# Opening of a transformer trunk: adaLN map loaded by column quarters, context projected as quarters land, token squares summed by TensorE

## Chip, cores and metric

One core of a Trainium2 chip (trn2) runs the whole program. The metric is the device time of one execution in microseconds; of several runs the median is taken. Engines: PE is TensorE (PEld its weight loads), DVE is VectorE, ACT is ScalarE, POOL is GpSimd, SP is SyncE, which issues the DMAs here.

## The reference, cut to what matters

Two layers over 1024 latent tokens and 256 context tokens of 1024 channels, in fp32. Each layer is an attention and a gated convolutional FFN, each behind an RMS norm that is modulated by a vector (adaLN): one map `w_mod[i]` of 1024 x 6144 gives six vectors of 1024 channels for the latents (from `c`) and six for the context (from `c_ctx`). The change touches the start of layer 0:

```
mod = silu_c @ w_mod[i] + b_mod[i]
mod_c = silu_cc @ w_mod[i] + b_mod[i]
sh1, sc1, gt1, sh2, sc2, gt2 = jnp.split(mod[:, None, :], 6, axis=-1)
...
h = modulate(rmsnorm(x, g_attn[i]), sh1, sc1)        # h * (1 + scale) + shift
hc = modulate(rmsnorm(ctx, g_attn[i]), sh1c, sc1c)
q, k, v = attn_inputs(h, w_in, gq, gk, n_kv)          # h @ w_qkv, 1024 x 3072
q_c, k_c, v_c = attn_inputs(hc, w_in, gq, gk, n_kv, with_q=not last)
```

Before the first projection of layer 0 can start, the shift and scale vectors (the first 2048 of the 6144 columns of `w_mod[0]`, 8 MiB) must be there, and the tokens must be normalised and modulated.

## The kernel before, in words

Tokens lie transposed: 128 channels on the partitions, 8 channel tiles (k), and three chunks of tokens in the free dimension: chunk 0 and chunk 1 of 512 latents, chunk 2 of 256 context tokens. Every fp32 factor of a large matmul is split into a high part (fp32r) and a low part, and a product is three matmuls: hi x hi, lo x hi, hi x lo. For weights this gives `whi` (ACT) and `wlo` (DVE or POOL), for tokens `h0hi`, `h0lo`, and `h0chi`, `h0clo` for the context.

The order of the work is planned by `Sched` (line 61), a list scheduler that runs when the program is built. Each operation has an engine, an assumed duration, the tokens it reads and writes, a key (smaller goes first) and the buffers it takes and gives back. The planner plays the operations through and then emits them; `InOrder` (line 39) binds each engine to that order. So the order on an engine is fixed; at run time an instruction only waits for its own inputs, and all that stand behind it on its engine wait with it.

The opening is the planner `sa` (lines 787 to 932):

- DMA order: context tokens (two halves of 0.5 MiB), `cpad` (the two silu vectors), `bmod`, `gn`, latent chunk 0 (four quarters of 0.5 MiB), the map in eight tiles `wm` of 128 rows x 2048 columns (1 MiB each), three weight slabs of the first head pair (0.375 MiB), latent chunk 1 (four of 0.5 MiB), the fourth slab.
- `mod_mm` (297): for each row tile of the map and each of the two vectors, 4 matmuls of 256 columns into 32 partitions each; all eight row tiles are summed in PSUM, so no column of the result is complete before the last row tile. Then `cp` copies the two sums (`modsb`), PE transposes them (`modt`), and `mod_finish` (280) adds the bias and multiplies with the norm's gain into `modc`.
- `stats(c)` (842): ACT squares each of the 8 channel tiles of a chunk; DVE adds the eight squares into `nsum`; PE multiplies `nsum` with a column of 1/1024 (`invd`), one matmul of one column per 128 tokens (`nps`), 2 for the context and 4 for chunk 0. From that DVE and POOL make 1/sqrt (`nv`, `ny`, `nt`), DVE puts it on diagonals (`dg`), PE spreads it over the partitions (`nps<-dg,ones`), and DVE multiplies the tokens with it (`x<-x,nps`).
- `apply(c)` (899): per channel tile `x` is modulated (ACT or DVE), copied to the high part and subtracted for the low part. All wait for the whole `modc`.
- The four slabs are split into `whi` and `wlo`. Two tiles of the `wlo` ring hold the context tokens until then, so slabs 2 and 3 wait for the context's `h0clo`.

Then the planner `sc` plans layer 0's attention, from the time `T0` (1163) on: eight head pairs, each with q, k, v projections (`plan_na_qkv`, 973) of ten token tiles of 128 in the order context (8, 9), chunk 0 (0 to 3), chunk 1 (4 to 7), each 24 matmuls of 384 columns (`mm`), beside the attention of the pair. The context's projection thus begins after the opening. `plan_norm` (632) normalises chunk 1 meanwhile (`sums`, `n1v`, `n1y`, `t`, `n1lo`).

Of the kernel before, what the change touches and what calls it, by code (L numbers as in the profile page):

```python
# [11 lines left out]
F32 = mybir.dt.float32  # L12
# [5 lines left out]
P = 128  # L18
D = 1024
KT = 8  # L20
# [205 lines left out]
@with_exitstack  # L226
def trunk_kernel(ctx, tc, xperm, xseq, cc, wmod, bmod, gnorm, na_wqkv, na_gq, na_gk, na_bias, na_wo,
                 sw_wqkv, sw_gq, sw_gk, sw_sink, sw_wo, rope_c, rope_s, band, w_up, conv, w_down, out):
# [109 lines left out]
    def t_act(n):  # L338
        return 0.094 + n / 1200.0
# [448 lines left out]
    slabs = Slabs(na_wqkv, WL0)  # L788

    with tc.tile_pool(name="x0", bufs=1, reuse_waits="tile") as xp, \  # L790
            tc.tile_pool(name="lw0", bufs=2, reuse_waits="tile") as lw, \
            tc.tile_pool(name="ps0", bufs=1, space=PS, reuse_waits="tile") as ps:
        xs = [hpool.tile([P, KT, 512], F32, tag="hhi", name="x0", bufs=2),
              Parts([lo_part("x1", F32) for _ in range(4)], 2),
              Parts([wring.tile([P, 1024], F32, tag="wlo", name="x2").rearrange("p (k t) -> p k t", k=4) for _ in range(2)], 4)]
        h = [hi_lo("h0", 0), None, hi_lo("h0", 2)]


        sa = Sched(dict(raw=3, w=WBUFS, sq=2, nsum=1, n=2))
# [11 lines left out]
        accs, raws = [None] * 2, [None] * KT  # L811
        for kt in range(KT):
            def load(e, kt=kt):
                raws[kt] = xp.tile([P, 2, 1024], F32, tag="wm", name=f"wm{kt}", bufs=KT)
                dma.dma_start(raws[kt].rearrange("p v c -> p (v c)"), wmod[0, kt * P:(kt + 1) * P, 0:2 * D])

            def mm(e, kt=kt):
                for v in range(2):
                    if kt == 0:
                        accs[v] = ps.tile([P, 512], F32, tag="mod", name=f"mod{v}", bufs=2)  # L820
                    mod_mm(accs[v], kt, raws[kt][:, v, :], kt == 0, kt == KT - 1)
            sa.op("dma", t_mb, load, writes=[("wm", kt)], key=4 + kt)
            sa.op("pe", 0.86, mm, reads=[("wm", kt)], writes=[("acc", v) for v in range(2)], key=0)
        for v in range(2):
            J = {}

            def cp(e, v=v, J=J):
                J["sb"] = xp.tile([P, 256], F32, tag="modsb", name="modsb0", bufs=2)
                act.activation(J["sb"], accs[v][:, :256], AF.Copy)

            def tr(e, v=v, J=J):
                J["gen"] = mod_finish(0, v, J["sb"], lambda: ps.tile([P, 512], F32, tag="modt", name="modt", bufs=2))
                next(J["gen"])

            def fin_(e, J=J):
                for _ in J["gen"]:
                    pass
            sa.op("act", 0.28, cp, reads=[("acc", v)], writes=[("sb", v)], key=-1)
            sa.op("pe", 0.43, tr, reads=[("sb", v)], writes=[("modt", v)], key=-1)
            sa.op("dve", 0.2 + 0.2 * v, fin_, reads=[("modt", v), ("bmod",), ("gn",)], writes=[("modc", v)], key=-1)  # L840

        def stats(c, key):
# [5 lines left out]
            for k in range(KT):  # L848
                def sq(e, k=k):
                    J["s", k] = lw.tile([P, 512], F32, tag="sq" if k else "nsum", name="sq" if k else "nsum", bufs=2 if k else 1)  # L850
# [4 lines left out]
                sa.op("act", t_act(n), sq, reads=[("x", c, k)], writes=[("sq", c, k)] if k else [("sums", c)], key=key + k,  # L855
                      acq=[("sq", ("sq", c, k), 1)] if k else [("nsum", ("nsum", c), 1)])
                if k:
                    sa.op("dve", t_dve(n), add, reads=[("sq", c, k), ("sums", c)], writes=[("sums", c)], key=key + k,
                          rel=[("sq", c, k)])

            def mp(e):
                J["mp"] = ps.tile([P, 512], F32, tag="n", name="nps", bufs=2)
                for i in range(nt):
                    pe.matmul(J["mp"][:, i:i + 1], J["s", 0][:, i * P:(i + 1) * P], invd, start=True, stop=True)
            sa.op("pe", 0.22 * nt, mp, reads=[("sums", c)], writes=[("mp", c)], key=key, acq=[("n", ("mp", c), 1)],
                  rel=[("nsum", c)])

# [14 lines left out]
            def dg(e):  # L882
                J["dg"] = lw.tile([P, 512], F32, tag="sq", name="dg", bufs=2)
# [35 lines left out]
        stats(0, 30)  # L919
        apply(2, 50)  # L920
        apply(0, 60)
        slabs.n_ahead = 4
        for j in range(4):

            free = [("h", 2, k) for k in range(4 * (j - 2), 4 * (j - 1))] if j > 1 else []
            sa.op("dma", 0.94, lambda e, j=j: slabs.load(j), writes=[("raw", j)], key=20 + j if j < 3 else 40,
                  acq=[("raw", ("raw", j), 2)])
            sa.op("act", t_act(768), lambda e, j=j: slabs.hi(j), reads=[("raw", j)] + free, writes=[("wh", j)],
                  key=50 + 2 * j, acq=[("w", ("w", j), 1)], rel=[("raw", j)])
            sa.op("dve", 0.87, lambda e, j=j: slabs.lo(j, e), reads=[("raw", j), ("wh", j)] + [("modc", 1)] * (j > 0),  # L930
                  writes=[("wl", j)], key=50 + 2 * j, rel=[("raw", j)])
        sa.run()
# [5 lines left out]

    def ps_alloc(pool_):

        return lambda tag, dt: pool_.tile([P, 512], dt, tag=tag, name=tag, bufs=PSB[tag])

    psa = ps_alloc(ps)
    SBUFS, PTB = 5, 2
# [28 lines left out]
    def plan_na_qkv(n):  # L973
# [188 lines left out]

    T0 = max(sa.at(("h", 2, 0)), sa.at(("wl", 0)))
    for tok, was in ([(("h0", c, k), ("h", c, k)) for c in (2, 0) for k in range(KT)] + [(("x1", k), ("x", 1, k)) for k in range(KT)]
                     + [(("wl", j), ("wl", j)) for j in range(4)]):
# [5 lines left out]
    for hp in range(HP):  # L1171
        for j in range(4):
            if 4 * hp + j >= slabs.n_ahead:
                slabs.plan(sc, 4 * hp + j, NT * hp + QKEY, NT)
            else:
                sc.hold("w", ("w", j), NT)
        for k in range(NT):
# [49 lines left out]
    plan_oproj0()  # L1227
    sc.run({e: max(0.0, sa.free.get(e, 0.0) - T0) for e in ("act", "dve", "pool")})
    ph.close()
# [878 lines left out]
    ps = ph.enter_context(tc.tile_pool(name="psa1", bufs=1, space=PS, reuse_waits="tile"))  # L2108
    psa = ps_alloc(ps)
    
    kkl1 = fin.tile([P, T], F32R, name="kkl1")
# [286 lines left out]
def layout(i):  # L2398
# [7 lines left out]
    a["cc"] = np.stack([cols(i["c"][0]), cols(i["c_ctx"])], axis=-1)  # L2406
    a["wmod"] = i["w_mod"]
    a["bmod"] = i["b_mod"].reshape(2, 6, 8, P).transpose(3, 0, 1, 2)
    a["gnorm"] = np.stack([i["g_attn"], i["g_ffn"]], 1).reshape(2, 2, 8, P).transpose(3, 0, 1, 2)
# [14 lines left out]
    for g in range(NKV):  # L2424
# [16 lines left out]

_INS = ["xperm", "xseq", "cc", "wmod", "bmod", "gnorm", "na_wqkv", "na_gq", "na_gk", "na_bias", "na_wo",
        "sw_wqkv", "sw_gq", "sw_gk", "sw_sink", "sw_wo", "rope_c", "rope_s", "band", "w_up", "conv", "w_down"]
# [22 lines left out]
```

## Time and profile before

| what | value |
|---|---|
| median of 3 runs | 2849.25 us (2848.09 to 2849.77) |
| the profiled execution | 2851.74 us |
| its span on the core | 2850.0 us |
| mean granted clock of TensorE | 0.989 |
| busy PE, DVE, ACT, POOL | 2784.4, 2324.1, 1713.2, 400.1 us |

The page of the profile gives sums over the span; a row of the view by stretches gives the busy time of each engine, the granted clock and the DMA share between two times; a row of the timeline gives start, duration, engine, line, operation, output<-input, partitions x columns and the count of merged instructions, and in brackets the idle time before it and what ended that. Nearly all operations bear line 51, the line of the helper that records them; so they are told apart by the names of their tiles.

### The profile page before, as it was taken

Reading aid. Unit: us, or ns where it says so; the run is one execution under the profiler, and the core shown is the slowest. Engines: PE = TensorE matmul, PEld = TensorE weight load, DVE = VectorE, ACT = ScalarE, POOL = GpSimd, SP = SyncE. Lnnn points to the kernel's source line nnn. Section 1 sums busy time; section 2 is a strip of 40 time slices with the busy share of each in tenths; the row PEclk is TensorE's granted clock in tenths of the full one; section 3 lists DMA queues with packets and bytes.
Section 4 is the critical chain, followed back from the end, with each engine's and each line's share of the span. In section 5 each row is a group of like instructions: output and inputs, shape, how many; then the busy total and the mean of one; then the engine's idle time right before and its main releaser. Section 6 shows DMA issues by size and latency. Waiting matters only on the chain.

```text
span 2850.0 us, 46124 instructions
## 1 busy us (share of the span) xinstructions
PE 2784.4 (98%) x16344; PEld 2455.3 (86%) x16344; DVE 2324.1 (82%) x5243; ACT 1713.2 (60%) x3382; POOL 400.1 (14%) x675
## 2 busy tenths in 40 slices
PE   6999999999999999999999999999999999999999
PEld 5999999998789987777788888999987788888887
DVE  7888888888688687877797787999987988888757
ACT  5877777778456554444454457888873554455443
POOL 1222212223000000000010006455520000000000
PEclk9999999999999999999999999999999999999999
DMA  6222222314745544444375551010234323324745
GB/s 247 65 95 80 83 67 75 96 60 125 250 142 192 183 162 140 154 142 160 135 258 194 181 169 29 13 34 16 73 128 138 116 105 111 111 93 149 253 148 182
DMA packets 140953, 367.20 MB, mean 129 GB/s; under 512 B 21425, under 2 KB 34225, under 8 KB 139313
## 3 DMA queue, kind: packets, MB, share of 16 engines
q1 hardware_dynamic: 140720, 364.25, 38.1%
q8 instruction: 129, 2.11, 0.3%
q14 instruction: 104, 0.84, 0.1%
HBM read 297.21 MB, written 66.98 MB: 128 GB/s over the span
## 4 chain that ended last, share of the span: by engine, by line
PE 69%; DVE 4%; ACT 2%; issue 1%; DMA 1%; DVEq 0%; ACTq 0%; SPq 0%
PE ua L51 17%; PE dn L51 15%; PE uc L51 13%; PE mm L51 6%; PE oacc L51 4%; PE ud L51 4%; PE pt L51 3%; PE pv L51 2%; PE dnc L51 2%; PE s L51 2%; DVE S L51 1%; PE mod L51 1%; ACT S L51 1%; DVE ptlo L51 1%; DVE x L51 0%
## 5 line engine op out<-in xcount | busy, mean ns | idle before, releaser
L51 ACT ACTIVATE whi<-wraw 128x512 fp32r<-128x512 f32 (+1 forms) x264 | 212.6, 806 | 203.6 <-PE uc L51 62.7
L51 DVE TENSOR_TENSOR wlo<-wraw,whi 128x512 fp32r<-128x512 f32 (+1 forms) x264 | 239.2, 907 | 45.3 <-ACT whi L51 44.8
L51 DVE TENSOR_TENSOR ptlo<-pt,pthi 128x512 fp32r<-128x512 f32 (+2 forms) x384 | 223.2, 595 | 48.6 <-ACT pthi L51 45.0
L51 PE MATMUL dn<-ghi,wlo 128*128 128x512 f32 x616 | 242.4, 394 | 0.0
L51 PE MATMUL dn<-ghi,whi 128*128 128x512 f32 x616 | 242.4, 394 | 0.0
L51 PE MATMUL dn<-glo,whi 128*128 128x512 f32 x616 | 242.3, 393 | 0.0
L51 ACT ACTIVATE pthi<-pt 128x512 fp32r<-128x512 f32 (+2 forms) x384 | 195.1, 524 | 71.1 <-PE pt L51 61.1
L51 ACT ACTIVATE S<-S,m 128x640 f32<-128x640 f32 (+3 forms) x288 | 220.8, 768 | 22.7 <-DVE m L51 19.6
L51 DVE SCALAR_TENSOR_TENSOR u<-c,cv,u 128x1023 f32<-128x1023 f32 x176 | 223.2, 1279 | 6.8 <-ACT u L51 5.8
L51 ACT ACTIVATE whi<-s 128x1024 fp32r<-128x1024 f32 (+1 forms) x120 | 113.3, 945 | 191.4 <-PE uc L51 137.4
L51 ACT ACTIVATE ghi<-graw 128x512 fp32r<-128x512 f32 x154 | 96.4, 631 | 190.2 <-PE dn L51 108.4
L51 PE MATMUL pt<-idr,S 128*128 128x128 f32 x1280 | 199.2, 278 | 6.8 <-DVE sm L51 2.6
L51 PE MATMUL mm<-whi,h0hi 128*128 128x384 f32 x512 | 181.1, 354 | 0.4 <-ACT qraw L51 0.4
L51 DVE TENSOR_TENSOR glo<-graw,ghi 128x512 fp32r<-128x512 f32 x154 | 105.4, 688 | 83.8 <-ACT ghi L51 76.4
L51 PE MATMUL mm<-wlo,h0hi 128*128 128x384 f32 x512 | 172.3, 337 | 0.0
L51 PEld LDWEIGHTS pt<-idr,S 128*128 128x128 f32 x1280 | 153.5, 143 | 17.4 <-DVE ptlo L51 3.9
L51 DVE TENSOR_TENSOR wlo<-s,whi 128x1024 fp32r<-128x1024 f32 (+1 forms) x120 | 129.6, 1080 | 40.6 <-ACT whi L51 40.5
L51 POOL TENSOR_TENSOR qy<-qv,mhalf 128x4 f32<-128x4 f32 (+2 forms) x120 | 126.2, 1052 | 227.0 <-DVE qv L51 197.0
L51 PE MATMUL pv<-ptlo,v 128*128 128x256 f32 (+1 forms) x688 | 153.9, 297 | 1.2 <-DVE ptlo L51 1.2
L51 PE MATMUL pv<-pthi,v 128*128 128x256 f32 (+1 forms) x688 | 147.7, 287 | 4.1 <-DVE osb L51 3.0
L51 PE MATMUL ua<-t12hi,whi 128*128 128x512 f32 x352 | 138.7, 394 | 5.5 <-ACT t12hi L51 3.9
L51 POOL TENSOR_TENSOR n1y<-n1v,mhalf 128x4 f32<-128x4 f32 (+1 forms) x9 | 9.2, 1025 | 953.3 <-DVE n1v L51 950.7
(315 smaller groups left out, 8906.4 us busy)
## 6 DMA issues: line engine op xcount, KB each, us to landing
wraw<-in_w_up_dram SPq DMA_DIRECT2D x132, 512.0 KB, 3.4
wm<-in_wmod_dram SPq DMA_DIRECT2D x80, 512.0 KB, 4.0
wraw<-in_w_down_dram SPq DMA_DIRECT2D x44, 512.0 KB, 3.5
graw<-g_dram SPq DMA_DIRECT2D x44, 512.0 KB, 4.4
wraw<-in_w_down_dram SPq DMA_DIRECT2D x88, 256.0 KB, 3.0
graw<-g_dram SPq DMA_DIRECT2D x66, 256.0 KB, 2.8
slab<-in_na_wqkv_dram SPq DMA_DIRECT2D x32, 384.0 KB, 3.7
woraw<-in_na_wo_dram SPq DMA_DIRECT2D x24, 512.0 KB, 4.4
```

What stands on the lines that cost most here:

```text
L51: r = f(*a, **k)
```

## The change

The first 2048 columns of layer 0's map are laid out anew on the host (`wmod0`) as four quarters: quarter q holds, for all 1024 rows, columns 256q to 256q+255 of both shift and scale. A quarter (2 MiB) is loaded in two halves of 4 row tiles, 8 KB a partition as before. When a quarter is in, its two channel tiles (2q and 2q+1) of shift and scale are complete: 16 matmuls per quarter (even and odd row tiles in different partition groups, added later by DVE), a copy, two transposes, five DVE operations. `apply` for channel tile k waits for quarter k // 2 alone. The DMA order is context, slab 0, quarter 0, chunk 0, slab 1, quarter 1, slab 2, quarter 2, slab 3, quarter 3, chunk 1.

The context tiles 8 and 9 of head pair 0 are projected within the opening: for each slab j (channel tiles 2j, 2j+1) 12 matmuls as soon as slab j and the modulated channel tiles are there, into two PSUM banks (`psq`) that the attention goes on with; `plan_na_qkv` leaves them out. Chunk 0 follows as before.

The squares are not added by DVE: PE multiplies each square tile with `invd` and sums over the 8 channel tiles in PSUM; 4 square buffers instead of 2 and a sum. The context tokens get tiles of their own, outside the `wlo` ring. In the order that results on PE, 16 one-column matmuls of the context stand first, then 8 of quarter 0, the context's broadcast, 8 of quarter 0, 4 one-column matmuls of chunk 0, the transposes of quarter 0, 24 one-column matmuls of chunk 0, 8 of quarter 1, the last 4 one-column matmuls, then projections of the context in four parts among the rest of the quarters.

```diff
+        SQB = 4
+        sa = Sched(dict(raw=3, w=WBUFS, sq=SQB, n=2, mod=2, modt=2))
-        for c, parts, key in ((2, 2, 0), (0, 4, 2), (1, 4, 30)):
+        for c, parts, key in ((2, 2, 0), (0, 4, 6), (1, 4, 30)):
...
+        def plan_quarter(q):
+            J = {}
+            for hf in range(2):
+                def load(e, hf=hf):
+                    if hf == 0:
+                        J["raw"] = xp.tile([P, KT, 2, 256], F32, tag="wm", name=f"wm{q}", bufs=4)
+                    dma.dma_start(J["raw"][:, 4 * hf:4 * hf + 4].rearrange("p k v c -> p (k v c)"),
+                                  wmod0[q, :, 2048 * hf:2048 * hf + 2048])
+                sa.op("dma", t_mb, load, writes=[("wm", q, hf)], key=4 + 4 * q + 0.5 * hf)
+                def mm(e, hf=hf):
...
+                    for kt in range(4 * hf, 4 * hf + 4):
+                        for v in range(2):
+                            g = 2 * v + kt % 2
+                            pe.matmul(J["acc"][32 * g:32 * g + 32, :256], cpad[:, kt, :], J["raw"][:, kt, v, :],
+                                      start=kt < 2, stop=kt > 5, skip_group_check=True)
...
-                def add(e, k=k):
-                    dve.tensor_tensor(out=J["s", 0][:, :n], in0=J["s", 0][:, :n], in1=J["s", k][:, :n], op=ALU.add)
+                def mp(e, k=k):
...
+                    for i in range(nt):
+                        pe.matmul(J["mp"][:, i:i + 1], J["s", k][:, i * P:(i + 1) * P], invd, start=(k == 0 and i == 0),
+                                  stop=(k == KT - 1), skip_group_check=True)
+                sa.op("act", t_act(n), sq, reads=[("x", c, k)], writes=[("sq", c, k)], key=key + k, acq=[("sq", ("sq", c, k), 1)])
+                sa.op("pe", 0.22 * nt, mp, reads=[("sq", c, k)], writes=[("mp", c)], key=key + k,
+                      acq=[("n", ("mp", c), 1)] if k == 0 else (), rel=[("sq", c, k)])
...
-                sa.op(("act", "dve"), (t_act(n) + 0.19, 0.07 + 0.8 * n / 960), mod, reads=[("modc", 0), ("modc", 1)],
+                sa.op(("act", "dve"), (t_act(n) + 0.19, 0.07 + 0.8 * n / 960), mod, reads=[("modc", k // 2)],
...
-        apply(2, 50)
+        apply(2, 28)
...
+            for tt in (8, 9):
+                def mm(e, j=j, tt=tt):
...
+                    for kt in (2 * j, 2 * j + 1):
+                        wh, wl = [a[:, kt % 2, :] for a in slabs.get(j)]
+                        for i, (a, w) in enumerate(((hh, wh), (hl, wh), (hh, wl))):
+                            pe.matmul(first_acc[tt][:, :384], a[:, kt, sl], w, start=(kt == 0 and i == 0),
+                                      stop=(kt == KT - 1 and i == 2))
+                sa.op("pe", 6 * t_pe(384), mm, reads=[("wl", j), ("h", 2, 2 * j), ("h", 2, 2 * j + 1)], writes=[("qa", tt)],
+                      key=60)
...
-        plan_qkv_mm(sc, key, psa, h, tt, slabs, hp, J, 0, ("h0", tt // 4) if hp == 0 else None)
+        if n < 2:
+            J["acc"] = first_acc[tt]
+            sc.hold("mm", I + ("acc",), 1)
+        else:
+            plan_qkv_mm(sc, key, psa, h, tt, slabs, hp, J, 0, ("h0", tt // 4) if hp == 0 else None)
...
-    T0 = max(sa.at(("h", 2, 0)), sa.at(("wl", 0)))
+    T0 = sa.at(("qa", 8))
```

More of the change, by code (lines that the diff above doesn't have):

```diff
@@ L794, in trunk_kernel @@
               Parts([lo_part("x1", F32) for _ in range(4)], 2),
-              Parts([wring.tile([P, 1024], F32, tag="wlo", name="x2").rearrange("p (k t) -> p k t", k=4) for _ in range(2)], 4)]
+              Parts([xp.tile([P, 4, 256], F32, name=f"x2{i}") for i in range(2)], 4)]
         h = [hi_lo("h0", 0), None, hi_lo("h0", 2)]
-        sa = Sched(dict(raw=3, w=WBUFS, sq=2, nsum=1, n=2))
+        SQB = 4
+        sa = Sched(dict(raw=3, w=WBUFS, sq=SQB, n=2, mod=2, modt=2))
         t_mb = 2.45
-        for c, parts, key in ((2, 2, 0), (0, 4, 2), (1, 4, 30)):
+        for c, parts, key in ((2, 2, 0), (0, 4, 6), (1, 4, 30)):
             t0, n = CH[c]
@@ L810, in trunk_kernel @@
         sa.op("dma", 0.5, lambda e: dma.dma_start(cv, conv), writes=[("cv",)], key=50)
[L811 to L817, printed above, removed]
-                for v in range(2):
[L819 to L823, printed above, removed]
@@ L842, in stats @@
+        for q in range(4):
+            plan_quarter(q)
         def stats(c, key):
@@ L849, in sq @@
                 def sq(e, k=k):
-                    J["s", k] = lw.tile([P, 512], F32, tag="sq" if k else "nsum", name="sq" if k else "nsum", bufs=2 if k else 1)
+                    J["s", k] = lw.tile([P, 512], F32, tag="sq", name="sq", bufs=SQB)
                     act.activation(J["s", k][:, :n], x[:, k, :], AF.Square)
-                def add(e, k=k):
-                    dve.tensor_tensor(out=J["s", 0][:, :n], in0=J["s", 0][:, :n], in1=J["s", k][:, :n], op=ALU.add)
[L855 to L866, printed above, removed]
+                def mp(e, k=k):
+                    if k == 0:
+                        J["mp"] = ps.tile([P, 512], F32, tag="n", name="nps", bufs=2)
+                    for i in range(nt):
[4 more added lines that the diff above has]
+                      acq=[("n", ("mp", c), 1)] if k == 0 else (), rel=[("sq", c, k)])
             def v(e):
@@ L1227, in trunk_kernel @@
     plan_oproj0()
-    sc.run({e: max(0.0, sa.free.get(e, 0.0) - T0) for e in ("act", "dve", "pool")})
+    sc.run({e: max(0.0, sa.free.get(e, 0.0) - T0) for e in ("pe", "act", "dve", "pool")})
     ph.close()
```

73 lines of the change are left out of this document (44 added, 29 removed).

## The prediction

> **What bounds the kernel now.** I read the page first, then the busy time by stretch, then the instructions of the first 60 us in order of time.
>
> ```profile
> PE 2784.4 (98%) x16344; PEld 2455.3 (86%) x16344; DVE 2324.1 (82%) x5243; ACT 1713.2 (60%) x3382; POOL 400.1 (14%) x675
> ```
>
> The page: TensorE (PE) is busy for 98% of the span. The next view gives, for a stretch, its length, busy time and count of PE, weight loads, DVE, ACT and POOL, then the granted clock, the DMA share and GB/s.
>
> ```profile
> 20.00:30.00 10.00, 9.02 (x88) 5.85 (x84) 6.38 (x20) 0.00 (x0) 1.02 (x1) 1.00 1.02 424
> ...
> 200.00:250.00 50.00, 50.00 (x373) 48.11 (x372) 36.37 (x138) 33.43 (x91) 10.87 (x16) 1.00 0.22 67
> ```
>
> At 20 to 30 us the DMA engines are full (share 1.02, 424 GB/s); at 200 to 250 us PE is never idle. So whatever the opening gains or loses shifts a stream that PE bounds, and nothing later absorbs it by itself. The opening on PE:
>
> ```profile
> 10.40 1.01 PE L51 MATMUL nps<-invd,nsum 128*128 128x1 f32 x4 [10.40 <-DVE nsum L51]
> 15.72 1.94 PE L51 MATMUL mod<-wm,cpad 128*32 128x256 f32 x16 [4.31 <-DMA wm<-in_wmod_dram]
> ...
> 19.98 1.87 PE L51 MATMUL nps<-invd,nsum 128*128 128x1 f32 x8
> 21.71 1.20 PE L51 MATMUL nps<-dg,ones 128*128 128x128 f32 x4
> 22.84 3.18 PE L51 MATMUL mod<-wm,cpad 128*32 128x256 f32 x32
> 26.62 1.13 PE L51 MATMUL nps<-dg,ones 128*128 128x128 f32 x8 [0.60 <-DVE dg L51]
> 27.68 1.93 PE L51 MATMUL mod<-wm,cpad 128*32 128x256 f32 x32
> 30.54 1.07 PE L51 MATMUL mod<-wm,cpad 128*32 128x256 f32 x16 [0.93 <-DMA wm<-in_wmod_dram]
> 34.03 1.07 PE L51 MATMUL mod<-wm,cpad 128*32 128x256 f32 x16 [2.42 <-DMA wm<-in_wmod_dram]
> 36.15 1.12 PE L51 MATMUL modt<-idr,modsb 128*128 128x128 f32 x4 [1.04 <-ACT modsb L51]
> 38.86 0.66 PE L51 MATMUL mm<-whi,h0chi 128*128 128x384 f32 x1 [1.60 <-DVE h0chi L51]
> ```
>
> ```profile
> 49.02 0.33 PE L51 MATMUL mm<-whi,h0hi 128*128 128x384 f32 x1
> ```
>
> The last MiB of the adaLN map lands at 34.0; its matmuls end at 35.1, the context projection runs from 38.86 to 49.02, and there the latent tiles (h0hi) begin. Before 34 PE waits for DMA: the transfer bounds the opening, and PE has room to spare. A fp32 matmul of the program is two rows here.
>
> The rows also show two speeds: 32 rows of mod take 3.18 us at 22.84 and 1.93 at 27.68. When the clock rises is read from stretches of 3.41 us (the steps in which it changes):
>
> ```profile
> 15.18:18.60 3.42, 2.42 (x24) 0.94 (x28) 2.75 (x6) 1.41 (x3) 0.00 (x0) 1.00 1.01 424
> 18.60:22.01 3.41, 3.41 (x25) 2.37 (x18) 0.12 (x1) 0.00 (x0) 0.00 (x0) 1.00 1.02 428
> ...
> 32.25:35.66 3.41, 1.07 (x16) 0.42 (x16) 0.41 (x1) 0.68 (x1) 0.00 (x0) 1.00 1.03 405
> 35.66:39.08 3.42, 1.34 (x5) 0.97 (x5) 2.94 (x12) 2.74 (x7) 0.00 (x0) 0.50 1.02 406
> 39.08:42.49 3.41, 3.41 (x11) 3.23 (x12) 3.41 (x10) 3.41 (x8) 0.00 (x0) 0.50 1.05 387
> ...
> 1684.30:1687.71 3.41, 3.41 (x18) 3.41 (x17) 3.02 (x7) 2.32 (x6) 0.00 (x0) 0.50 1.00 327
> 1687.71:1691.12 3.41, 3.41 (x13) 3.41 (x13) 1.92 (x11) 0.94 (x4) 1.16 (x2) 0.50 0.76 293
> ```
>
> ```profile
> 1684.23 0.41 PE L51 MATMUL mm<-whi,h1clo 128*128 128x128 f32 x1
> ```
>
> After 31% busy (32.25) the clock falls to 0.50; after one stretch full of 384-column matmuls (39.08) it is 1.00 again. But 1684.30 is also 100% busy, with 128-column matmuls paced by their weight loads (PEld 3.41), and is followed by another stretch at 0.50. And 18.60, fully busy, 1.87 us of it one-column nps, is followed by the slow mod at 22.84 (before 25 us the column says 1.00, but no change is recorded there; the durations decide). So PE that only loads weights does not raise the clock.
>
> **The change, part by part.** Weights (DMA): the map comes in eight 1 MiB halves of quarters, in lines of 8 KB as before. The queue holds, up to the last half, context 1 MiB, latents 2, map 8 and now all four slabs (1.5): 12.5 MiB instead of 11. At 424 GB/s a MiB takes 2.47 us. The first MiB of the map was used at 15.72, after 4 MiB; so the halves land at about 11.6 and 14.1, 22.4 and 24.9, 28.3 and 30.7, 34.1 and 36.6 (up to 1 us later, as the last one was before: 34.0 against 32.9 by this rate). Cost by itself: 2.6 to 3.6 us on the last half. The later tokens (x1) end at most 0.9 later, unneeded until the latent tiles run.
>
> Sums of squares: DVE's 14 additions go; nothing but this sum waited for DVE there, so the gain is nothing. In their place PE gets, for each of 8 k, 2 matmuls (context) and 4 (latents) of one column with the squares as weights: 48 instead of 6. Price: 1.87 us for 8 rows, that is 0.47 a matmul; at full clock the same form costs half:
>
> ```profile
> 60.41 1.02 PE L51 MATMUL pt<-invd,sums 128*128 128x1 f32 x8
> ```
>
> The plan books 0.22 each. 48 cost 22.4 us at half clock, 12.2 at full, and PE takes its instructions in order, so everything placed behind them waits: in the changed order the 24 for k = 1 to 6 of the latents stand ahead of quarter 1's first matmul.
>
> Which clock? By the stretches above one-column matmuls do not raise it and let it fall after one stretch. I take half clock until a run of 384-column matmuls. Then, from the squares of the context:
>
> ```profile
> 6.31 0.71 ACT L51 ACTIVATE sq<-x 128x256 f32<-128x256 f32 x2
> ```
>
> the first pair of sums is done before; seven pairs from 6.8, 6.6, to 13.4; half quarter 0, 1.94, to 15.3; wait for dg 0.6 (an estimate: POOL's power and DVE's small operations, less this mod); broadcast 1.2, to 17.1; second half, to 19.0; latents k = 0, 1.87, to 20.9; transposes 0.55; k = 1 to 6, 11.2, to **32.7**; quarter 1's first half (landed at 22.4!) to 34.6; k = 7 to 36.5. So PE, not the DMA, now bounds the opening. Next 6 projections 1.95 (0.32 each), mod 1.94, 6 more: 42; between 39.3 and 42.7, by where the 3.41 us steps fall, the clock rises. At full clock: transposes, mod 1.07, to 43.1; the broadcast of the latents' norm, 1.13, to **44.2** (before: 27.7); mod 1.07, 12 projections 2.1, transposes, last quarter 2.14: about 50 (before: 35.1).
>
> Then ACT and DVE. The latents' normalisation, in DVE's idle time before, now falls into its fullest stretch:
>
> ```profile
> 27.79 4.87 DVE L51 TENSOR_TENSOR x<-x,nps 128x512 f32<-128x512 f32 x8 [0.72 <-PE nps L51]
> ```
>
> ```profile
> L51 DVE TENSOR_TENSOR h0lo<-x,h0hi 128x512 fp32r<-128x512 f32 x8 | 5.2, 679 | 0.0
> L51 DVE TENSOR_TENSOR wlo<-slab,whi 128x768 fp32r<-128x768 f32 x4 | 3.8, 947 | 3.2 <-ACT whi L51 3.2
> L51 DVE TENSOR_TENSOR h0clo<-x,h0chi 128x256 fp32r<-128x256 f32 x8 | 3.1, 410 | 0.0
> L51 DVE TENSOR_SCALAR x<-x,modc 128x512 f32<-128x512 f32 x5 | 2.6, 533 | 0.0
> L51 DVE TENSOR_SCALAR x<-x,modc 128x256 f32<-128x256 f32 x5 | 1.9, 402 | 0.0
> L51 DVE CAST h0chi<-x 128x256 fp32r<-128x256 f32 x5 | 1.2, 281 | 0.0
> ...
> L51 DVE TENSOR_TENSOR modc<-modt,bmod_t 128x8 f32<-128x8 f32 x4 | 0.5, 161 | 0.2 <-PE modt L51 0.2
> ```
>
> Still to do on DVE at 44.2: normalisation 4.9, h0lo 5.2, h0clo of six k 2.4, one wlo 0.9, two quarters of modc (ten operations of 0.16) 1.6, some six context operations 2.0, one modulation and cast of 512 columns 0.9: 17.9, to 62; without the overlap of neighbours' ends some 61. Before, the last h0lo ended at 53.4:
>
> ```profile
> 52.74 0.68 DVE L51 TENSOR_TENSOR h0lo<-x,h0hi 128x512 fp32r<-128x512 f32 x1
> ```
>
> So DVE is 7.8 us late, and the context projection, whose last 12 matmuls wait for quarter 3's operations behind that DVE queue, ends near 59 instead of 49.0. PE is then 10 late, but waits less for DVE afterwards:
>
> ```profile
> PEld mm L51 <- DVE n1lo L51: 3.5, 5, 1.4
> ```
>
> Of these waits and that for the last h0lo I take 2 to 2.5 back. Net **+7.5 us**, bounds +3 (the clock rises once in 15 to 22 us: 3.4 us of PE at double speed, and 1 more given back) and +11.5 (it falls again while PE waits for DVE at 50 to 57, and nothing comes back).
>
> At nothing: modsb and transposes twice as often (four ACT copies, 0.55 us of PE each pair; counted above); the token tiles outside the weight ring (slabs 2 and 3 no longer wait for h0clo; they are ready early either way); two PSUM banks kept for the projection; the rest of layer 0 planned anew from other times, the same instructions, PE never idle: 2 us either way, in the bounds.
>
> **Sum.** The profiled execution took 2851.74 us (span 2850.0), 2.5 above the median of the three timed runs, 2849.25. 2851.74 + 7.5 = 2859.2 for such an execution; for the median 2849.25 + 7.5 = **2856.8**.
>
> **Rivals.** *PE keeps up (faster).* If a busy PE of any kind raised the clock, it would be at full speed from about 12 us. The same list then gives: context sums to 12.8, quarter 0 done by 17.0, latents k = 0 to 6 done by 24.2, quarter 1 by 28.4, and from there the DMA leads: last half at 36.6 to 37.6, mod 1.07, the step from mod's end to the first projection as before (35.1 to 38.86) 3.8, last 12 projections 2.1: 43.6 to 44.6 instead of 49.0, so -4.9, **2844.3**. It decides from the point at which the 24 one-column matmuls run at 0.24 instead of 0.47. For it: PE is busy all the while. Against: the stretches 18.60 and 1684.30. The Trainium skill, "TensorE: Matmul & The Clock Gate", section "What's actually happening", says the full clock comes after one busy window of about 3.4 us; with busy as this profile counts it, that rule would give this rival. This trace disagrees at 1684.30, 3.41 of 3.41 us busy and the clock still 0.50. Chance 0.16.
>
> *It evens out (no change).* The clock rises early for one step (-3.4), and DVE's waits after the opening go (-3.5): +7.5 becomes about +1, **2850**. For it: two mod runs and the broadcast fill most of 15.2 to 18.6. Against: PE also waits 0.6 us for dg there, and a stretch 71% busy with mod (15.18 to 18.60, rows 15.72 and on) did not raise it before. Chance 0.10.
>
> *The change does not do what it says:* in the forecast itself quarters are not used as they land; quarter 1 waits 10 us on PE.
>
> **How the numbers follow.** Forecast 0.74, its own range 2852 to 2861.5; 0.2% is 5.7 us, about what a measurement of this kernel can tell from no change. Of the 0.74, 0.58 lies above +5.7 and 0.16 below. The second rival's 0.10 is within; of the first's 0.16, 0.10 is within and 0.06 beyond -5.7. So slower 0.58, same 0.36, faster 0.06. The range takes the forecast's, the second rival's and the upper edge of the first's: 2846 to 2861.5.
>
> **What would show it.** Right: about 96 rows nps<-invd,sq of 0.23 us each; mod of quarter 1 starting near 32, ten us after its landing; granted clock 0.50 until 39 or later; the first h0hi matmul at 56 to 60, the last h0lo ending at 58 to 62. Wrong: nps at 0.13 us, mod rows that end a wait for DMA in quarters 2 and 3, h0hi at 44 to 46. If h0hi starts late and the time is unchanged, the loss was given back between 60 and 90 us.

## The result, and the profile after

The changed kernel takes **2857.51 us** (median of 10 runs, 2853.31 to 2859.80); the kernel before, run beside it, 2850.09 us (10 runs, 2848.09 to 2854.41). The ratio is 1.002, 95% interval 1.001 to 1.0029, so some 3 to 8 us: slower by 7.4 us in the medians and by 5.8 in the means, where +7.5 was forecast. The profiled execution took 2857.97 us (span 2855.9, mean granted clock 0.987), 6.2 us over that of before. The sum is right and its parts are not: the opening lost 5 us and not 10, and the 2 to 2.5 us that were to come back did not. (In the rows below, nps holds the sums of squares, mod the map, mm the projections.)

The page's row of busy time, and the row of 200 to 250 us from the view by stretches, of the changed kernel:

```profile
PE 2800.4 (98%) x16432; PEld 2471.1 (87%) x16432; DVE 2318.6 (81%) x5238; ACT 1719.8 (60%) x3389; POOL 401.0 (14%) x675
```

```profile
200.00:250.00 50.00, 50.00 (x380) 48.04 (x379) 38.36 (x137) 35.37 (x93) 11.38 (x17) 1.00 0.24 77
```

PE has 88 rows and 16 us more, and is still never idle at 200 us: what the opening loses is not made up there. The opening on PE, from the timeline of the changed kernel:

```profile
7.15 6.13 PE L51 MATMUL nps<-invd,sq 128*128 128x1 f32 x28 [1.04 <-ACT sq L51]
13.21 1.93 PE L51 MATMUL mod<-wm,cpad 128*32 128x256 f32 x16
15.23 1.22 PE L51 MATMUL nps<-dg,ones 128*128 128x128 f32 x4
16.39 1.28 PE L51 MATMUL mod<-wm,cpad 128*32 128x256 f32 x16
...
18.76 8.93 PE L51 MATMUL nps<-invd,sq 128*128 128x1 f32 x48
27.62 1.93 PE L51 MATMUL mod<-wm,cpad 128*32 128x256 f32 x16
...
38.66 1.16 PE L51 MATMUL nps<-dg,ones 128*128 128x128 f32 x8
...
43.26 1.93 PE L51 MATMUL mod<-wm,cpad 128*32 128x256 f32 x32
...
51.54 0.44 PE L51 MATMUL mm<-whi,h0chi 128*128 128x384 f32 x1 [2.19 <-DVE h0chi L51]
...
54.12 0.33 PE L51 MATMUL mm<-whi,h0hi 128*128 128x384 f32 x1
```

No mod row waits for a transfer: PE, and not the DMA, bounds the opening until 45 us; from there PE waits for the context's tokens (2.19 us before 51.54). The 48 rows of one column hold quarter 1 back until 27.62. The latents' first matmul comes at 54.12 (before 49.02). The view by stretches of the changed kernel, cut at the steps of its clock (length, busy PE, PEld, DVE, ACT, POOL, then the granted clock):

```profile
13.45:16.86 3.41, 3.32 (x28) 1.56 (x24) 1.36 (x8) 0.46 (x1) 0.71 (x1) 1.00 1.01 413
16.86:20.27 3.42, 3.42 (x40) 2.90 (x33) 3.28 (x14) 2.71 (x7) 0.00 (x0) 1.00 1.05 425
20.27:23.69 3.42, 3.42 (x18) 3.42 (x18) 2.47 (x6) 2.67 (x5) 0.00 (x0) 0.50 1.00 412
23.69:27.10 3.41, 3.41 (x17) 3.41 (x18) 0.00 (x0) 0.06 (x1) 0.00 (x0) 0.50 1.03 420
...
33.93:37.34 3.41, 3.41 (x22) 2.30 (x15) 0.96 (x5) 0.38 (x1) 0.00 (x0) 0.50 1.00 412
37.34:40.75 3.41, 3.41 (x43) 1.95 (x41) 2.80 (x11) 1.34 (x2) 0.00 (x0) 1.00 1.03 409
```

The step from 13.45, full of mod and a broadcast, is followed by one step at full clock (40 rows instead of 18; the column says 1.00 until the first change is recorded, at 20.27, so here the rows decide). In that step PE goes over to one-column matmuls, and the clock falls again until 37.34. That mod rows raise the clock was there to be seen before: in the kernel before, the step from 22.01, most of it mod, was followed by mod at full speed (32 rows in 1.93 us at 27.68):

```profile
22.01:25.42 3.41, 3.41 (x31) 1.81 (x33) 2.51 (x9) 0.00 (x0) 1.02 (x1) 1.00 1.01 423
```

DVE, from the timeline of the changed kernel:

```profile
40.16 1.88 DVE L51 TENSOR_TENSOR x<-x,nps 128x512 f32<-128x512 f32 x3
...
55.12 0.83 DVE L51 TENSOR_TENSOR h0lo<-x,h0hi 128x512 fp32r<-128x512 f32 x1
```

The last h0lo ends at 55.95 (before 53.42). The chunk-1 waits, from the view of waits of the changed kernel, 44 to 130 us:

```profile
PEld mm L51 <- DVE n1lo L51: 3.3, 6, 1.2
...
PEld mm L51 <- ACT h0hi L51: 1.1, 1, 1.1
```

Before, these were 3.5 and 0.4 us: in these waits nothing came back. How far the shift carries is read from the transposes klt, one set per head pair: count, shortest/median/longest, then the start of the first and of the last. The tile's row, first of before, then of the changed kernel:

```profile
L51 PE MATMUL pt<-idr,klt x160: 221/250/328, 64.3 to 681.9; 128*128 128x128 f32 x160
```

```profile
L51 PE MATMUL pt<-idr,klt x160: 221/250/328, 68.7 to 687.2; 128*128 128x128 f32 x160
```

4.4 us late at the first, 5.3 at the last. Behind 690 us the clock differs from one execution to the next (from 690 to 790 us its mean was 0.97 in the profiled execution and 1.00 in r_after_again, the same kernel), so the time of one run says less than these rows.

### The profile page after: what moved, and what is told of

Its sections match the earlier page's. It is cut to its first block, busy times and chain, and to the rows that moved or that the text cites. A ratio compares the mean times of both kernels' runs of the same rounds, so it can differ in the third digit from the quotient of the medians.

```text
span 2855.9 us, 46284 instructions
## 1 busy us (share of the span) xinstructions
PE 2800.4 (98%) x16432; PEld 2471.1 (87%) x16432; DVE 2318.6 (81%) x5238; ACT 1719.8 (60%) x3389; POOL 401.0 (14%) x675
## 4 chain that ended last, share of the span: by engine, by line
PE 89%; DVE 5%; ACT 2%; DMA 1%; issue 1%; DVEq 0%; SPq 0%; ACTq 0%
PE ua L51 17%; PE mm L51 16%; PE dn L51 15%; PE uc L51 13%; PE pt L51 7%; PE pv L51 5%; PE s L51 5%; PE oacc L51 4%; PE ud L51 4%; PE dnc L51 2%; DVE S L51 1%; PE mod L51 1%; DVE ptlo L51 1%; ACT S L51 0%; DVE x L51 0%
```

## The experiments

Theory: one-column matmuls in TensorE's order cost twice their price since they do not raise the clock, and hold the quarters back. Rivals: the quarters themselves or their order cost the time; DVE's queue does; or the planner's low prices (0.22 and 0.9) put the work in a bad order. One table first, since the experiments are read by the same three marks: the start of the first h0hi matmul, of the last klt, and the time beside before in the same group of runs, on one chip (ratio with its 95% interval). The ratio is taken over all runs and can differ from the quotient of the two medians, by up to 0.0006 here. Times of different groups are compared by their distance to before.

| kernel | first h0hi, us (to before) | last klt, us (to before) | median, us (runs) | before, us | ratio |
|---|---|---|---|---|---|
| before | 49.02 | 681.9 | 2850.09 (10) | | |
| after | 54.12 (+5.1) | 687.2 (+5.3) | 2857.51 (10) | 2850.09 | 1.002 (1.001 to 1.0029) |
| r_after_again | 53.63 (+4.6) | 688.1 (+6.2) | 2851.70 (1) | 2850.73 | |
| e1_dve_sums | 48.29 (-0.7) | 680.9 (-1.0) | 2849.38 (11) | 2851.47 | 0.9993 (0.9984 to 1.0002) |
| e2_pe_sums_alone | 53.45 (+4.4) | 687.4 (+5.5) | 2854.65 (11) | 2851.47 | 1.0008 (0.9999 to 1.0017) |
| e3_true_prices | 64.73 (+15.7) | 701.3 (+19.4) | 2869.15 (5) | 2851.47 | 1.006 (1.0047 to 1.0072) |
| e4_pairs | 52.44 (+3.4) | 687.3 (+5.4) | 2856.65 (11) | 2851.47 | 1.002 (1.0011 to 1.0028) |
| e5_fill | 46.80 (-2.2) | 678.6 (-3.3) | 2845.61 (11) | 2850.73 | 0.9984 (0.9976 to 0.9993) |
| r_e5_again | 46.49 (-2.5) | 678.0 (-3.9) | 2848.18 (10) | 2850.48 | 0.9986 (0.9976 to 0.9996) |
| e6_ctx_on_pe | 48.41 (-0.6) | 684.3 (+2.4) | 2852.56 (11) | 2850.73 | 1.0005 (0.9996 to 1.0014) |
| e7_wide | 47.11 (-1.9) | 681.4 (-0.5) | 2851.08 (11) | 2850.73 | 1.0 (0.9991 to 1.0009) |
| e8_wide_fill | 46.23 (-2.8) | 681.1 (-0.8) | 2850.71 (12) | 2850.48 | 1.0 (0.9991 to 1.0008) |
| r_e8_again | 45.49 (-3.5) | 680.9 (-1.0) | 2849.47 (12) | 2849.96 | 0.9995 (0.9986 to 1.0004) |
| e9_plan | 45.95 (-3.1) | 677.5 (-4.4) | 2845.73 (12) | 2849.96 | 0.9981 (0.9972 to 0.999) |

### Sums back on DVE (e1_dve_sums)

```diff
-                    for i in range(nt):
-                        pe.matmul(J["mp"][:, i:i + 1], J["s", k][:, i * P:(i + 1) * P], invd, start=(k == 0 and i == 0), ...
+                def add(e, k=k):
+                    dve.tensor_tensor(out=J["s", 0][:, :n], in0=J["s", 0][:, :n], in1=J["s", k][:, :n], op=ALU.add)
```

> The changed kernel with the sums of squares as before: DVE adds the eight squares, 6 one-column matmuls instead of 48; quarters, slab order and the early context projection stay. Theory (48 one-column matmuls at half clock make PE the bound of the opening): quarter 1's first mod matmul starts where its data land, near 22 to 25 us instead of 27.6; the last quarter's near 36 to 38; first latent matmul (h0hi) at 47 to 50; time 6 to 10 us under the changed kernel, 0 to 3 us under the kernel before. Rival A (the extra 1.5 MiB of slabs ahead of the last quarter is the cost): within 2 us of the changed kernel. Rival B (the finer operations crowd DVE and ACT): more work on DVE, so no faster than the changed kernel.

The rest of the change stays. From the timeline of PE:

```profile
24.95 2.73 PE L51 MATMUL mod<-wm,cpad 128*32 128x256 f32 x32
...
30.59 1.07 PE L51 MATMUL mod<-wm,cpad 128*32 128x256 f32 x16 [0.65 <-DMA wm<-in_wmod_dram]
...
35.22 1.07 PE L51 MATMUL mod<-wm,cpad 128*32 128x256 f32 x16 [1.20 <-DMA wm<-in_wmod_dram]
...
40.85 0.38 PE L51 MATMUL modt<-idr,modsb 128*128 128x128 f32 x2
43.87 0.69 PE L51 MATMUL mm<-whi,h0chi 128*128 128x384 f32 x1 [2.64 <-ACT h0chi L51]
```

Without the sums PE waits for the transfer again, and the loss is gone (ratio 0.9993 against 1.002). So the sums on PE cost the time and the quarters do not: without them the quarters bring 0.7 to 1 us by the marks, and the interval of the time touches 1. DVE has its additions back and the time falls, so DVE's queue is not the cost either. What limits them shows in the last rows: the transposes of quarter 3 stand behind twelve projections, then PE idles 2.64 us.

### Sums on PE alone (e2_pe_sums_alone)

The kernel before, with the squares summed by one-column matmuls as in the change, and nothing else of it.

```diff
-                def add(e, k=k):
-                    dve.tensor_tensor(out=J["s", 0][:, :n], in0=J["s", 0][:, :n], in1=J["s", k][:, :n], op=ALU.add)
+                    for i in range(nt):
+                        pe.matmul(J["mp"][:, i:i + 1], J["s", k][:, i * P:(i + 1) * P], invd, start=(k == 0 and i == 0), ...
```

> The kernel before with one part of the change: the squares summed by 48 one-column matmuls; map by rows, one modc, context projected later, as before. Theory: 24 of these matmuls of the latents stand ahead of the first mod; mod starts near 23 to 25 us (before 15.7), the last mod ends at 41 to 43 (before 35.1), the first latent matmul at 54 to 56 (before 49.0); time 4 to 7 us over the kernel before. Rival A and B (transfer order, or crowding by quarters, is the cost): within 1.5 us of the kernel before, as PE had room under the transfers.

Timeline of PE, then the stretches of this kernel:

```profile
6.78 16.38 PE L51 MATMUL nps<-invd,sq 128*128 128x1 f32 x76 [0.82 <-ACT sq L51]
23.09 1.93 PE L51 MATMUL mod<-wm,cpad 128*32 128x256 f32 x16
```

```profile
11.31:14.73 3.42, 3.42 (x18) 3.42 (x18) 0.78 (x5) 1.90 (x4) 0.71 (x1) 1.00 1.02 429
14.73:18.14 3.41, 3.41 (x18) 3.41 (x18) 0.00 (x0) 1.25 (x3) 0.00 (x0) 1.00 1.01 425
18.14:21.55 3.41, 3.41 (x18) 3.41 (x18) 0.00 (x0) 1.24 (x2) 0.00 (x0) 1.00 1.01 420
```

PE is busy without a gap for 16.38 us, and the 16 rows of mod behind that still take 1.93 us, the half-clock time (1.07 at full). (The column says 1.00 because no change is recorded yet.) The sums alone put the opening 4.4 us late and the last klt 5.5: nearly the whole loss of the change, without its quarters. The time, +3.2 us in the medians (4 to 7 expected) with an interval that touches 1, is less sharp than the marks.

### True prices for the planner (e3_true_prices)

```diff
-                sa.op("pe", 0.9, mm, reads=[("wm", q, hf)], ...
+                sa.op("pe", 1.94, mm, reads=[("wm", q, hf)], ...
-                sa.op("pe", 0.22 * nt, mp, reads=[("sq", c, k)], ...
+                sa.op("pe", 0.47 * nt, mp, reads=[("sq", c, k)], ...
```

> The changed kernel, with two planned durations set to those measured at half clock: 0.47 us instead of 0.22 for a one-column matmul, 1.94 instead of 0.9 for half a quarter. The work is the same, the order on PE is another: mod goes ahead of the one-column matmuls, the broadcast of the latents' norm goes behind 36 context projections. Theory (it is the load on PE, not its order): the mod matmuls follow their landing within 3 us, but the broadcast comes at 48 us or later (changed kernel 38.7) and the first latent matmul at 56 or later; time 2 to 8 us over the changed kernel. Rival C (the load fits, only the misjudged prices put the matmuls in a bad order): 3 us or more under the changed kernel.

The mods now follow their landings, but the sums of the latents are pushed behind everything, their broadcast to 56.06 us and h0hi to 64.73. It is 17.7 us over before, where the changed kernel was 7.4 over: 10 us worse, more than the 2 to 8 expected. So the rival of the low prices fails for this order: better-informed prices are no cure. That no order would be one is not shown.

### Half of the sums (e4_pairs)

```diff
+                def add(e, k=k):
+                    dve.tensor_tensor(out=J["s", k][:, :n], in0=J["s", k - 1][:, :n], in1=J["s", k][:, :n], op=ALU.add)
...
+                if k % 2:
```

> The changed kernel with half the one-column matmuls: DVE adds the squares in pairs (8 additions), PE sums four pair sums, 24 matmuls. Theory: the loss follows the count while PE is behind the transfers: quarter 1's first mod at 24 to 27 us, first latent matmul 2 to 5 us earlier than in the changed kernel; time 2 to 6 us under the changed kernel and not faster than with all sums on DVE by more than 1 us. Rivals A and B: within 1.5 us of the changed kernel.

DVE adds pairs, PE sums 24 columns instead of 48. Timeline of PE, then stretches of this kernel:

```profile
25.54 1.93 PE L51 MATMUL mod<-wm,cpad 128*32 128x256 f32 x16
...
48.32 0.44 PE L51 MATMUL mm<-whi,h0chi 128*128 128x384 f32 x1 [2.19 <-DVE h0chi L51]
```

```profile
45.53:48.94 3.41, 1.13 (x6) 0.55 (x4) 3.31 (x13) 2.40 (x4) 0.00 (x0) 1.00 0.92 324
48.94:52.35 3.41, 3.41 (x11) 3.41 (x12) 3.41 (x8) 2.83 (x8) 0.00 (x0) 0.50 0.18 71
```

Quarter 1 starts 2.1 us earlier, as expected. But the wait for quarter 3's tokens empties a step (1.13 of 3.41 us), and the last 12 projections run at half clock: of the gain 1.7 us is left in the opening (2 to 5 expected) and nothing at the last klt. The time, 0.9 us under that of the changed kernel or 2.2 by the distance to before, is too near to tell the theory (2 to 6) from the rivals (within 1.5); it is the start of quarter 1 that follows the count.

### The last pair of projections later (e5_fill, r_e5_again)

e1_dve_sums, with one dependency more: the projections of slab 2 wait for the transposes of quarter 3, so that these no longer stand behind them and the 12 projections fill PE's wait for the tokens.

```diff
-                sa.op("pe", 6 * t_pe(384), mm, reads=[("wl", j), ("h", 2, 2 * j), ("h", 2, 2 * j + 1)], ...
+                sa.op("pe", 6 * t_pe(384), mm, reads=[("wl", j), ("h", 2, 2 * j), ("h", 2, 2 * j + 1)] + [("modt", 3)] * (j == 2), ...
```

> The kernel with the sums on DVE and the quarters kept (e1_dve_sums), and one more dependency: the 12 context projections of the third pair of channel tiles wait for the transposes of the last quarter, so they fill PE's wait for the last quarter's operations (in e1_dve_sums they stood ahead of those transposes, PE then idled 2.6 us and the last 12 ran at half clock from 43.9 to 48.3). Theory: the last transposes near 39 to 40 us instead of 40.9, the clock stays up, first latent matmul at 44 to 46 instead of 48.3; time 2 to 5 us under e1_dve_sums, 3 to 6 us under the kernel before. Rival (the latents' operations on DVE and ACT set the end of the opening, whatever PE does): within 1 us of e1_dve_sums.

> The fastest version so far (e5_fill) once more beside it on one chip: 2 to 7 us under the kernel before if its first result holds; within 1 us of the kernel before if that was the luck of the clock's steps.

Timeline of PE in e5_fill:

```profile
38.80 0.44 PE L51 MATMUL modt<-idr,modsb 128*128 128x128 f32 x2 [0.50 <-ACT modsb L51]
42.25 0.44 PE L51 MATMUL mm<-whi,h0chi 128*128 128x384 f32 x1 [0.93 <-DVE h0chi L51]
...
46.80 0.45 PE L51 MATMUL mm<-whi,h0hi 128*128 128x384 f32 x1 [1.43 <-ACT qraw L51]
```

The transposes come 2 us earlier than in e1, and the wait for h0chi shrinks from 2.64 to 0.93 us; h0hi, which then waits for ACT's qraw, starts at 46.80 where 44 to 46 was expected. In both groups it is faster than before: 0.9984 and 0.9986. The change's quarters, with this order, thus have a gain, of 2 to 5 us.

### Only the context's sums on PE (e6_ctx_on_pe)

DVE adds the latents' squares; the 16 one-column matmuls of the context stay.

```diff
+            if c == 2:
...
+                        pe.matmul(J["mp"][:, i:i + 1], J["s", k][:, i * P:(i + 1) * P], invd, ...
+            else:
...
+                    dve.tensor_tensor(out=J["s", 0][:, :n], in0=J["s", 0][:, :n], in1=J["s", k][:, :n], op=ALU.add)
```

> The changed kernel with the latents' squares added by DVE, and only the context's 16 one-column matmuls kept on PE. Theory (what costs is the 24 and 4 of the latents, ahead of quarter 1; the context's 16 end near 13.4 us, while PE has nothing else until 11.5): mod of quarter 1 starts near 22 to 24 us; time within 2 us of e1_dve_sums, 6 to 10 us under the changed kernel. Rival (each one-column matmul costs the same, wherever it stands): a third of the loss stays, so 2 to 3 us over e1_dve_sums.

The opening is that of e1 (48.41 against 48.29): the context's sums put the first half of quarter 0 back (12.92 against 11.17) but not quarter 1 (24.90 against 24.95), and cost the opening nothing. The time missed the expectation: it is 3.9 us over e1 by the distance to before, where at most 2 was expected, and by itself it would speak for the rival, that each one-column matmul costs the same. But the loss comes after the opening. The stretches of this kernel tell where:

```profile
72.13:75.55 3.42, 1.87 (x7) 1.11 (x7) 3.42 (x7) 2.14 (x4) 0.00 (x0) 1.00 0.00 0
75.55:78.96 3.41, 2.76 (x9) 1.92 (x9) 3.40 (x19) 2.98 (x8) 1.01 (x1) 0.50 0.01 2
```

PE waits in the stage where chunk 1 is normalised (68 to 90 us), and the clock falls for three steps. That stage was planned anew from the opening's other times. That this is the cause was not tried for e6 itself; e9 below takes it up.

### The same sums with a wide operand (e7_wide)

The order of the change, the same number of matmuls; the moving operand has 128 equal columns instead of one.

```diff
+    invw = cpool.tile([P, P], F32, name="invw")
+    dve.memset(invw, 1.0 / D)
-                        pe.matmul(J["mp"][:, i:i + 1], J["s", k][:, i * P:(i + 1) * P], invd, ...
+                        pe.matmul(J["mp"][:, i * P:(i + 1) * P], J["s", k][:, i * P:(i + 1) * P], invw, ...
```

> The changed kernel with the same order on every engine; only the moving operand of the 48 sums is 128 equal columns instead of one. Weights and count are the same. If it is the half clock that makes the sums dear and streamed columns raise it: granted clock 1.00 from 9 to 14 us on, about 0.14 us a row (as the broadcast of that shape takes at full clock), quarter 1's mod near 22 to 24 us, first latent matmul 45 to 49, time 5 to 10 us under the changed kernel. If 128 columns do not raise it either: 0.30 us a row (the same broadcast at half clock) instead of 0.22, some 6 us more of PE in the opening, and time 4 to 8 us over the changed kernel. If the sums are hidden after all (rivals A and B): within 1.5 us.

Timeline of PE, then stretches of this kernel:

```profile
6.80 6.06 PE L51 MATMUL nps<-invw,sq 128*128 128x128 f32 x28 [0.61 <-ACT sq L51]
12.78 1.07 PE L51 MATMUL mod<-wm,cpad 128*32 128x256 f32 x16
...
18.02 5.52 PE L51 MATMUL nps<-invw,sq 128*128 128x128 f32 x48
24.32 1.07 PE L51 MATMUL mod<-wm,cpad 128*32 128x256 f32 x16 [0.78 <-DMA wm<-in_wmod_dram]
...
38.77 1.07 PE L51 MATMUL mod<-wm,cpad 128*32 128x256 f32 x16 [1.38 <-DMA wm<-in_wmod_dram]
```

```profile
9.01:12.42 3.41, 3.41 (x18) 3.41 (x17) 0.96 (x1) 1.52 (x3) 0.00 (x0) 1.00 1.00 401
12.42:15.84 3.42, 2.46 (x32) 1.47 (x34) 1.41 (x7) 0.00 (x0) 0.71 (x1) 1.00 1.00 413
```

This decides it. 28 rows, nearly all at half clock, take 6.06 us, one-column rows 6.13: no cost of the width is seen. The step from 9.01 has the same busy PE and PEld as those of e2, yet mod behind it takes 1.07 us: the clock has risen. The 48 rows then take 5.52 us instead of 8.93, quarters 1 to 3 wait for DMA, and h0hi starts 7.0 us before that of the changed kernel. The time is 0.3 us over before instead of 7.4 (1.0 against 1.002). More arithmetic in the same places made the kernel faster; so the half clock is what the sums cost.

### Wide sums and the later pair (e8_wide_fill, r_e8_again)

e7_wide with the dependency of e5_fill (both diffs above).

> The changed kernel whole, sums of squares on PE with the 128-column moving operand (e7_wide), and the dependency of e5_fill. Theory (the clock was the cost, not the place of the sums): the opening as in e5_fill, first latent matmul at 44.5 to 47 us, time 2 to 5 us under e7_wide and within 2.5 us of e5_fill, so 3 to 6 us under the kernel before. Rival (48 matmuls on PE cost also at full clock): within 1 us of e7_wide.

> The kernel e8_wide_fill once more, on the chip of e9_plan, for that comparison: under each theory within 1 us of its first time, ratio to before 1.000.

The opening gains as expected (-2.8 and -3.5 us at h0hi), the time does not: 1.0 and 0.9995, where e7 has 1.0. By itself that fits the rival (the sums cost also at full clock); the opening does not, and e9 below, with the same sums, refutes it. Between h0hi and the last klt 2 to 2.5 us are lost again. The stretches of e8_wide_fill show a place, with PE waiting and the clock down:

```profile
68.07:71.48 3.41, 2.22 (x10) 1.42 (x9) 3.41 (x6) 1.48 (x3) 0.00 (x0) 1.00 0.00 0
71.48:74.89 3.41, 1.67 (x7) 0.94 (x6) 3.41 (x12) 2.13 (x4) 0.00 (x0) 0.83 0.00 0
74.89:78.30 3.41, 1.98 (x6) 1.48 (x6) 3.14 (x14) 3.40 (x11) 0.00 (x0) 0.50 0.01 2
```

### Layer 0's order as before (e9_plan)

e8_wide_fill, with the planner of layer 0 told that PE is free when its plan starts. All of layer 0's attention is planned anew by that; PE's order in chunk 1's stage is then again that of the kernel before.

```diff
-    sc.run({e: max(0.0, sa.free.get(e, 0.0) - T0) for e in ("pe", "act", "dve", "pool")})
+    sc.run({e: max(0.0, sa.free.get(e, 0.0) - T0) for e in ("act", "dve", "pool")})
```

> The 128-column sums and the later third pair as in e8_wide_fill, and the planner of layer 0 told that TensorE is free at the start of its plan instead of at the end of the opening's; this puts the order of TensorE's groups there back to that of the kernel before (57, 4, 4, 15, 4, 4, 15, 4, 9 groups between the transposes). If the order of the stage around chunk 1's normalisation is what eats the gain of the opening: no half-clock step in 70 to 90 us, TensorE's wait for n1lo about 3.5 us instead of 4.6, a steady shift near -3 us behind the opening, and a time 2 to 4 us under e8_wide_fill. If the stage loses because its inputs come when they come (rival), whatever the order: waits and the half-clock step stay, and the time is within 1 us of e8_wide_fill.

The stretches, then the row of n1lo in the view of waits (44 to 130 us), which was 4.6, 6, 2.3 in both runs of e8; then the tile's row of klt, all of e9_plan:

```profile
68.07:71.48 3.41, 2.87 (x15) 2.56 (x16) 3.41 (x5) 1.76 (x5) 1.24 (x2) 1.00 0.00 0
71.48:74.89 3.41, 3.11 (x18) 2.79 (x17) 3.41 (x7) 2.05 (x3) 0.00 (x0) 1.00 0.00 0
74.89:78.30 3.41, 3.09 (x21) 2.46 (x19) 3.40 (x14) 3.34 (x8) 0.00 (x0) 1.00 0.01 2
```

```profile
PEld mm L51 <- DVE n1lo L51: 3.4, 5, 1.4
```

```profile
L51 PE MATMUL pt<-idr,klt x160: 220/250/284, 60.2 to 677.5; 128*128 128x128 f32 x160
```

The opening is that of e8; the half clock is gone, PE is busy for 9.07 us of those three stretches instead of 5.87, and the shift at the last klt is -4.4. The time is 3.7 us under r_e8_again on the same chip, and 0.9981 of before; that is not to be told apart from e5_fill's 0.9984. So the order that was made anew from the opening's times was what took the gain; the stretches put it into chunk 1's stage.

### The changed kernel once more (r_after_again)

> The changed kernel once more, unchanged, for a second trace: the steps of the clock fall elsewhere in each execution. Theory: if the clock does not rise between 15 and 20 us this time, quarter 1's mod starts near 31 to 33 us instead of 27.6 and the first latent matmul 2 to 5 us later than 54.1, with the time longer by as much; if it rises there again, the same times within 1 us.

The opening repeats within 0.5 us (53.63), and the last klt within 1 (+6.2). Its one time, 2851.70, does not repeat within the 1 us expected: it lies 1.6 us under the lowest of the ten runs, 1.0 us over before in its group, and what differs is behind layer 0's attention. One run cannot decide on changes of this size; the intervals and the marks can.

## Why the prediction was right, and where its parts were not

The mechanism was right: 48 one-column matmuls at half clock make PE the bound, and what stands behind them is late. The sizes of the steps were not, and that the sum came out within 0.1 us is luck.

- **PE becomes the bound, not the DMA: right.** Only from e1 and e7, where PE keeps up, are the landings seen: 24.3, 30.4, 32.8 and 38.8 (e7) where 22.4, 28.3, 30.7 and 36.6 (and up to 1 us more) were estimated. They were estimated 1 us too early at least, which cost the forecast nothing.
- **One-column matmuls do not raise the clock: right**, by e2 (16.38 us at half clock) and e7 (the same rows, wider, raise it). It is not the luck of one execution: in both traces of the changed kernel the 48 rows take 8.93 and 9.01 us, in all four with the wide operand (e7, e8 twice, e9) 5.52.
- **Price 0.47: somewhat high.** Long runs take 0.43 to 0.44 us a matmul (16.38 for 38, 6.13 for 14); the 1.87 us of eight rows that it was taken from holds an end that a longer run spreads out.
- **Half clock until a run of 384-column matmuls, so quarter 1 starts at 32.7: failed, 27.62.** Mod rows raised the clock too, as in the kernel before (step 22.01). The wait for dg, 0.6 us by the estimate, did not come; so the two mods and the broadcast filled the step 13.45 to 16.86, and the next ran at full clock. That is the case "the clock rises once in 15 to 22 us", which stood as a bound and as the second rival's first half. It gives 3.4 us; the rest is the wait, the price and the first pairs, which end at 13.2 and not 13.4.
- **The clock rises between 39.3 and 42.7: failed, 37.34**, since all was 5 us early. The latents' broadcast ended at 39.8 instead of 44.2.
- **DVE's remaining 17.9 us: right in size, wrong in place.** From 39.8 to 55.95 are 16.1 us; the forecast, less the overlaps that it took off, was 16.8 (44.2 to 61). It began 4.4 us early, so the last h0lo was 2.5 us late and not 7.8.
- **Context projection 10 us late: failed, 5.1.** The wait of its last 12 matmuls for quarter 3's tokens did come (2.19 us for h0chi), as forecast, but began and ended earlier, with DVE's work.
- **2 to 2.5 us given back: failed, none.** The waits for n1lo and h0hi grew from 3.9 to 4.4 us, and the clock fell for a step there. In the wide kernel the cause is shown (e8 against e9: the new order of chunk 1's stage). For the changed kernel itself that was not tried.
- **Sum +7.5: +7.4 in the medians, by luck.** Step by step the trace gives +5.1 in the opening and +5.3 at the last klt, +6.2 in the profiled execution; the means of the ten runs give +5.8. The two errors, 5 us too much in the opening and 2 to 2.5 us of return that is not there, cancel in part; the last 1 to 2 us are within what executions differ by, and no step of the forecast accounts for them. Of the signs named for "right", the 96 rows came as said (0.22 us each at half clock); the first h0hi (54.12, not 56 to 60), the last h0lo (55.95, not 58 to 62), quarter 1 (27.62, not near 32) and the clock (up at 37.34, not 39 or later, and once before) did not.
- **The rivals.** "PE keeps up" is refuted for this kernel. e7 shows that it needed only the wider operand; h0hi then starts at 47.11, not at 43.6 to 44.6: the landings come 2 us later, and PE waits 2.18 us for DVE's h0chi. "It evens out" had its first half come true (the early step) and not its second.

The rule of the Trainium skill that spoke for the first rival ("TensorE: Matmul & The Clock Gate", section "What's actually happening": full clock after one busy window of about 3.4 us) is, with busy as the profile counts it, borne out by e7, where one full step from 9.01 to 12.42 was enough, and contradicted by e2, where three such full steps in a row were not. The measurement decides: what PE does while busy matters here.

## What to carry to other kernels

Before small matmuls are moved onto an idle TensorE, read from the rows which clock they would run at: a busy engine with one-column operands stayed at half clock here, and as it works in order, it held back the map's quarter 1 (27.62 against 24.32 in e7). If such a sum must be there, a wider moving operand may be the cheaper one (6.06 against 6.13 us for 28 rows, and the clock rises). And where a planner orders later stages from the opening's times, compare that order too: in e8 a new order there cost 3 to 4 us of what the opening had gained, until e9 put the old one back.

## What the runs showed of the hardware

- **Width and the clock.** 128 equal columns took as long as one at half clock (0.22 us a row), and the clock rose after one full step of them; with one column it did not in 16.38 us. It even fell: the step 16.86 to 20.27 of the changed kernel, 3.42 of 3.42 us busy and most of it one-column rows, is followed by half clock. But the fp32r projections of 128 columns at 1684.30, in the prediction, did not raise it either, with the same busy PE and PEld. So by these rows neither busy time nor the number of columns alone decides; what is counted stays open.
- **When the clock falls.** A step with 1.87 us of projections busy (e6, 72.13) is followed by half clock, one with 2.46 (e7, 12.42) is not. Between these it is not settled: in the kernel before, a step with 1.86 us of mod (28.83) kept the full clock and the next, with 1.07 (32.25, in the prediction), lost it:

```profile
28.83:32.25 3.42, 1.86 (x32) 0.63 (x24) 3.42 (x7) 0.00 (x0) 0.00 (x0) 1.00 1.00 398
```
